# A two-layer encoder on one core: operands padded to multiples of 256 bytes, and softmax steps of paired heads in another order

## The chip, the cores and the metric

The kernel runs on one core of a Trainium2 chip. Its time is device microseconds (us) of that core. The shares, waits and durations below come from one profiled execution, as its own time says.

## What is computed

The reference is an encoder trunk of two layers on 512 tokens of width 1024, all in float32. Layer 0 mixes tokens by dilated attention in three groups, layer 1 by a bidirectional state-space layer; each is followed by a SwiGLU feed-forward of 2816 hidden units.

```python
def reference(x, ...):
    h = x
    for layer in range(DEPTH):                       # DEPTH = 2
        if layer % 2 == 0:
            h = h + dilated_attention_mixer(rms_norm(h, attn_norm), w_qkv, w_attn_out)
        else:
            h = h + s5_mixer(rms_norm(h, ssm_norm), w_ssm_in, ..., w_glu)
        h = h + swiglu_ffn(rms_norm(h, ffn_norm[layer]), w_ffn_in[layer], w_ffn_out[layer])
    return rms_norm(h, final_norm)
```

Attention has 16 heads of 64. For each head and group a banded softmax gives an output and a log-sum-exp; the groups' outputs are weighted by a softmax over the log-sum-exps and added.

## The kernel before

Every large product is three float32r matmuls: an operand is split in a high and a low part, and high x high, high x low and low x high are added in PSUM. `WStream` loads the weights in units of 128x1024 (512 KB); for each unit ScalarE writes the high part `whi` (L111) and VectorE the low part `wlo` (L112), up to two units ahead of their use. `gemm_a` (L742) then runs 24 matmuls of 128x512 for a unit, with the weights stationary and the activations moving: `X` (attention input and, later, attention output), `Y` (input of both feed-forwards and of the state-space layer), `hh`/`hl` in `hid0`, `yh`/`yl` in the pool `ssm`. Two places turn it round, with the weights moving: `emit_v` (L844, 256 columns) and the last product (L1511, 512 columns, with `hh`/`hl` of `hid1` stationary). By the code there are 5,280 float32r matmuls of 512 columns: 1,536 over `X` (64 units), 2,304 over `Y` (96 units), 528 over `hid0`, 384 over `ssm`, 528 at L1511; and 1,152 of 256 columns (768 at L844, 384 in attention).

Tiles come from pools on two sides of each partition. The left side grows up from `const`, with `w` (the weight units), `attn`, `Y`, `e1` and `hid1` behind it; the right side grows down from its top, with `hT` first and `X`, `hid0` and `ssm` below it. By the allocation of the kernel before, tiles of `w`, `attn` and `Y` start 96 bytes past a multiple of 256, those of `X`, `hid0` and the operands in `ssm` 224 bytes, and those of `hid1` 160 bytes.

Attention runs beside the projection of the next head pair. `plan` lists spans of projections: `qk` (7 units of 24 matmuls) and `v`. Each span has a list of pieces, (cost, function), and `Bg.tick` issues the next piece when the credit that the matmuls have earned passes half of its cost; the credit for a matmul is the span's total cost over its matmul time. So a piece's place in program order follows from the costs ahead of it. For an even head h and the odd h + 1, `A` holds the scores (`sc1` for group 1, `sc2` for groups 2 and 3 of both heads; each with the reductions of L892 and L913 on VectorE and the exponentials of L924 on ScalarE). `W` holds the four steps of `weigh`: part 0 is 16 small copies on GpSimd (L936), part 1 is three VectorE instructions (L941, L942) and an exponential, part 2 is four small VectorE instructions (L947 to L949) and the four scalings of `P2` (L951), part 3 is four scalings of `P1` on ScalarE (L954). `B` transposes the probabilities on TensorE (`tr`; L970 reads `P2`, L965 `P1`) and multiplies them by the values (`pv`, L989 and L1000). In the spans 2, 3, 6 and 9 (pairs that start with heads 0, 2, 6 and 10) scores and values of a pair share one span; the pairs 4, 8 and 12 have their scores in a `v` span and their values in the `qk` span behind it; the pair of heads 14 and 15 ends in `tailp`, whose first five pieces stand between the splits of the attention output (`xo`, L1072 on ScalarE and L1073, on GpSimd but for the first) and the rest beside its product (L1092).

Beside the first feed-forward (about 700 to 1,100 us) the same pieces mechanism builds the tables of the state-space layer on VectorE and GpSimd, with transposes at L445.

Of the kernel before, what the change touches and what calls it, by code (L numbers as in the profile page):

```python
# [7 lines left out]
F32 = mybir.dt.float32  # L8
# [5 lines left out]
P = 128  # L14
# [52 lines left out]
def fv(ap):  # L67
    return ap.bitcast(F32)
# [444 lines left out]
def build(tc, a, out):  # L513
# [62 lines left out]
    with ExitStack() as ctx:  # L576
        left = ctx.enter_context(tc.tile_pool(name="const", bufs=1, side="left"))
        wpool = ctx.enter_context(tc.tile_pool(name="w", bufs=3, side="left"))
        right = ctx.enter_context(tc.tile_pool(name="hT", bufs=1, side="right"))
# [13 lines left out]
        hT = [right.tile([P, S], F32, name=f"h{m}") for m in range(KT)]  # L593
        cols = left.tile([P, 64], F32, name="cols")

        def norm_tile(pool, i, m, src_psum=None):

            src = hT[m] if src_psum is None else src_psum
            hi = pool.tile([P, S], F32R, tag=f"hi{m}", name=f"xhi{m}")
            lo = pool.tile([P, S], F32R, tag=f"lo{m}", name=f"xlo{m}")  # L600
            nc.scalar.activation(out=hi, in_=src, func=ACTF.Copy, scale=gains[:, gcol[i], m:m + 1])
            nc.vector.scalar_tensor_tensor(out=lo, in0=src, scalar=gains[:, gcol[i], m:m + 1], in1=fv(hi),  # L602
                                           op0=ALU.mult, op1=ALU.subtract)
            return hi, lo
# [89 lines left out]
        for m in range(KT):  # L694
            if m == 5:
                ps = pso.tile([P, 2, S], F32, tag="o", name="xps")[:, 0, :]
            else:
                pool, tag = ((pss, "s"), (pst, "pt"), (psg, "g"), (pss, "s"))[m // 2]
# [175 lines left out]
        def sc1(h, bp):  # L874
            c = head(h)
            p, e = h // 2, h % 2
            QA, QB, QL = qk[p]["Q"]
            KK = qk[p]["K"][e]
            QQ, QL = (QA, QB)[e], QL[e]
            ps = pss.tile([P, 2, 256], F32, tag="s", name="sps")  # L880
            for j in range(2):
                b = 2 * bp + j
                i0, step = win[b]

                def kap(t):
                    return bass.AP(tensor=t.tensor, offset=t.offset + i0, ap=[list(t.ap[0]), [step, 2], [128, 4], [1, 32]])
                nc.tensor.matmul(ps[:, j, :], QQ[:, b * 128:(b + 1) * 128], kap(KK), start=True, stop=False)

                nc.tensor.matmul(ps[:, j, :], QL[:, b * 128:(b + 1) * 128], kap(KK), start=False, stop=True)
            for j in range(2):  # L890
                b = 2 * bp + j
                nc.vector.tensor_tensor_reduce(out=c.P1[:, b, :], in0=ps[:, j, :], in1=dist1[:, (0, 1, 1, 2)[b], :],  # L892
                                               scale=-SLOPES[h], scalar=-3e38, op0=ALU.add, op1=ALU.max,
                                               accum_out=c.st[:, b:b + 1])
            fin(c, c.P1, 2 * bp, 0)

        def sc2(p, rp):

            cc = [head(2 * p + e) for e in range(2)]
            q = qk[p]  # L900
            pp = [pss.tile([P, 2, 256], F32, tag="s", name="sps") for e in range(2)]
            for j in range(2):
                r = 2 * rp + j
                cs = slice(r * 128, (r + 1) * 128)
                for i, (nq, nk) in enumerate((("q2", "k2"), ("q3", "k3"))):
                    for e in range(2):
                        rows = slice(64 * e, 64 * e + 64)
                        nc.tensor.matmul(pp[e][:, j, 128 * i:128 * i + 128], q[nq][rows, cs], q[nk][rows, cs],
                                         start=True, stop=True)
            for e, c in enumerate(cc):  # L910
                for j in range(2):
                    r = 2 * rp + j
                    nc.vector.tensor_tensor_reduce(out=c.P2[:, r, :], in0=pp[e][:, j, :], in1=dist23,  # L913
                                                   scale=-SLOPES[2 * p + e], scalar=-3e38, op0=ALU.add, op1=ALU.max,
                                                   accum_out=c.st[:, 4 + r:5 + r])
                fin(c, c.P2, 2 * rp, 4)
# [39 lines left out]
        def tr(h, t):  # L956
            c = head(h)
            ps = pst.tile([P, S], F32, tag="pt", name="ptp")
            if t < 2:
                pv = ps.rearrange("p (t r b i) -> p t r b i", t=2, r=4, b=2)  # L960
                for u in range(2):
                    m = 2 * t + u
                    bs = ((m, 1), (m + 1, 0)) if m < 3 else ((0, 0), (3, 1))
                    for x, (b, half) in enumerate(bs):
                        nc.tensor.transpose(pv[:, u, :, x, :], c.P1[:, b, half * 128:half * 128 + 128], ident)  # L965
            else:
                for u in range(2):
                    r = 2 * (t - 2) + u
                    for g in range(2):
                        nc.tensor.transpose(ps[:, u * 256 + g * 128:u * 256 + g * 128 + 128],  # L970
                                            c.P2[:, r, g * 128:g * 128 + 128], ident)
            PT = ap_.tile([P, 2, S], F32R, tag="PT", name="PT", bufs=3)
            nc.scalar.activation(out=PT[:, 0, :], in_=ps, func=ACTF.Copy)  # L973
            nc.vector.tensor_tensor(out=PT[:, 1, :], in0=ps, in1=fv(PT[:, 0, :]), op=ALU.subtract)  # L974
            c.PT[t] = PT
# [33 lines left out]
        def A(h):  # L1009
            s = [(600, lambda: sc1(h, 0)), (600, lambda: sc1(h, 1))]  # L1010
            t = [(1200, lambda i=i: sc2(h // 2, i)) for i in range(2)]
            return s if h % 2 else [s[0], t[0], s[1], t[1]]

        def W(h):
            return [(c, lambda i=i: weigh(h, i)) for i, c in enumerate((1500, 1000, 1500, 1200))]

        def B(h):
            return [(700, lambda: tr(h, 2)), (700, lambda: tr(h, 3)), (700, lambda: tr(h, 0)), (600, lambda: pv(h, 2)),
                    (700, lambda: tr(h, 1)), (600, lambda: pv(h, 3)), (600, lambda: pv(h, 0)), (1000, lambda: pv(h, 1))]

        def mix(x, y):

            n = min(len(x), len(y))
            return [p for q in zip(x, y) for p in q] + x[n:] + y[n:]

        def scores(h):
            w, x = W(h), A(h + 1)
            return A(h) + [w[0], x[0], w[1], x[1], w[2], w[3]]

        def values(h):  # L1030
            return mix(B(h), W(h + 1)) + B(h + 1)

        spans = [[], [], scores(0) + values(0), scores(2) + values(2), scores(4), values(4), scores(6) + values(6),
                 scores(8), values(8), scores(10) + values(10), scores(12), values(12), A(14)]
        for st, pieces in zip(plan, spans):
            if st[0] == "qk":
                bg.span(pieces, 24 * MM * (st[3] - st[2]))
# [31 lines left out]
        def xo(m, eng):  # L1069
# [2 lines left out]
            nc.scalar.activation(out=hi, in_=oT[m], func=ACTF.Copy)  # L1072
            eng.tensor_tensor(out=lo, in0=oT[m], in1=fv(hi), op=ALU.subtract)  # L1073
            XO[m] = (hi, lo)
        tailp = mix(W(14), A(15)) + values(14)
        for m in range(KT - 1):
            xo(m, nc.gpsimd if m else nc.vector)
            if m < 5:
# [152 lines left out]
        sp = s0.enter_context(tc.tile_pool(name="ssm", bufs=1, side="right"))  # L1231
# [1 line left out]
        pY = s0.enter_context(tc.tile_pool(name="psY", bufs=2, space=PSUM))  # L1233
        pT = s0.enter_context(tc.tile_pool(name="psT", bufs=1, space=PSUM))
        p1 = s0.enter_context(tc.tile_pool(name="ps1", bufs=2, space=PSUM))
        Us = [sp.tile([P, 8, 66], F32, name=f"U{i}") for i in range(3)]
        for t in Us:
            nc.vector.memset(t[:, :, 0:1], 0.0)
            nc.vector.memset(t[:, :, 65:66], 0.0)
# [211 lines left out]
        e1 = f1.enter_context(tc.tile_pool(name="e1", bufs=1, side="left"))  # L1451
# [31 lines left out]
                nc.gpsimd.tensor_tensor(out=hv, in0=hv, in1=gfin[0], op=ALU.mult)  # L1483

        def fin_tok(q):
            sc = e1.tile([P, 8], F32, tag="fs", name="fs", bufs=2)
            y, r_, t = (sc[:, i:i + 1] for i in range(3))
            nc.vector.scalar_tensor_tensor(out=y, in0=ssum[:, q, 1:2], scalar=-0.5 / D, in1=ssum[:, q, 0:1],
                                           op0=ALU.mult, op1=ALU.add)
            nc.vector.tensor_scalar(out=r_.bitcast(I32), in0=y.bitcast(I32), scalar1=-0.5, scalar2=GUESS,  # L1490
                                    op0=ALU.mult, op1=ALU.add)
            for _ in range(3):
                nc.vector.scalar_tensor_tensor(out=t, in0=r_, scalar=y, in1=r_, op0=ALU.mult, op1=ALU.mult)
                nc.vector.scalar_tensor_tensor(out=r_, in0=t, scalar=1.5, in1=r_, op0=ALU.add, op1=ALU.mult)
            h0, h1 = (hrow[q][:, i * S:i * S + S] for i in range(2))
            nc.scalar.activation(out=h0, in_=h0, func=ACTF.Copy, scale=r_)
            nc.vector.scalar_tensor_tensor(out=h1, in0=h1, scalar=r_, in1=gfin[1], op0=ALU.mult, op1=ALU.mult)
            for l in range(2):
                nc.sync.dma_start(out=ov[2 * q + l], in_=hrow[q][64 * l:64 * l + 64, :])

        NK = HT // 2
        for fh in range(2):
# [11 lines left out]
            for kp in range(NK - last):  # L1514
                w = ws.get()
# [36 lines left out]
```

## Time and profile before

| | us |
|---|---|
| median of 3 runs | 1680.38 |
| their range | 1677.62 to 1685.16 |
| profiled execution, its own time | 1683.88 |
| its span, first to last instruction | 1682.1 |

TensorE's matmuls cover 93% of the span, VectorE 60%, ScalarE 39%, GpSimd 31%. A matmul's busy time reaches past the start of the next one, since matmuls are pipelined; how fast they follow each other is read from the distance of their starts, or from their count in a stretch that holds nothing else. The granted clock of TensorE is a share of full speed: 1.00 is 2.4 GHz, and near 0.5 is 1.2 GHz.

### The profile page before, as it was taken

Reading aid. Unit: us, or ns where it says so; the run is one execution under the profiler, and the core shown is the slowest. Engines: PE = TensorE matmul, PEld = TensorE weight load, DVE = VectorE, ACT = ScalarE, POOL = GpSimd, SP = SyncE. Lnnn points to the kernel's source line nnn. Section 1 sums busy time; section 2 is a strip of 40 time slices with the busy share of each in tenths; the row PEclk is TensorE's granted clock in tenths of the full one; section 3 lists DMA queues with packets and bytes.
Section 4 is the critical chain, followed back from the end, with each engine's and each line's share of the span. In section 5 each row is a group of like instructions: output and inputs, shape, how many; then the busy total and the mean of one; then the engine's idle time right before and its main releaser. Section 6 shows DMA issues by size and latency. Waiting matters only on the chain. (4 is left out here: it accounts for less than half of the span.)

```text
span 1682.1 us, 22587 instructions
## 1 busy us (share of the span) xinstructions
PE 1557.8 (93%) x8428; PEld 1278.0 (76%) x8428; DVE 1014.1 (60%) x1714; ACT 653.7 (39%) x1148; POOL 524.8 (31%) x788
## 2 busy tenths in 40 slices
PE   8988999999999899999988989888699999999997
PEld 6877888798797678776766767666578888888886
DVE  6366565565556688886777785568845434433223
ACT  5255454454454432344444443422133333332122
POOL 1022011010110340398888986344412110111010
PEclk9999999999999999999998999989899999999999
DMA  6222232222222142345655545658633233333332
GB/s 177 88 63 63 63 89 63 70 70 76 76 63 76 29 109 85 106 118 171 179 132 159 157 127 157 206 187 237 190 85 93 86 101 100 93 89 107 102 100 63
DMA packets 278669, 185.17 MB, mean 110 GB/s; under 512 B 39424, under 2 KB 260768, under 8 KB 276512
## 3 DMA queue, kind: packets, MB, share of 16 engines
q1 hardware_dynamic: 278128, 183.13, 37.3%
q8 instruction: 66, 1.08, 0.3%
q10 hardware_dynamic: 432, 0.60, 0.1%
q14 instruction: 43, 0.35, 0.1%
HBM read 154.34 MB, written 27.26 MB: 108 GB/s over the span
## 5 line engine op out<-in xcount | busy, mean ns | idle before, releaser
L112 DVE TENSOR_TENSOR wlo<-wraw,whi 128x1024 fp32r<-128x1024 f32 (+1 forms) x234 | 302.1, 1294 | 189.9 <-ACT whi L111 184.3
L111 ACT ACTIVATE whi<-wraw 128x1024 fp32r<-128x1024 f32 x238 | 241.5, 1019 | 260.5 <-PE ops L1511 76.3
L742 PE MATMUL gps<-xhi,whi 128*128 128x512 f32 x792 | 322.3, 407 | 0.0
L742 PE MATMUL gps<-xhi,wlo 128*128 128x512 f32 x792 | 313.9, 396 | 0.7 <-DVE wlo L112 0.7
L742 PE MATMUL gps<-xlo,whi 128*128 128x512 f32 x792 | 313.8, 396 | 0.5 <-DVE xlo L602 0.5
L936 POOL COPY st<-st 32x4 f32<-32x4 f32 x256 | 62.1, 243 | 475.8 <-ACT P L924 351.3
L742 PEld LDWEIGHTS gps<-xhi,wlo 128*128 128x128 f32 x792 | 150.7, 190 | 35.1 <-DVE wlo L112 1.2
L742 PEld LDWEIGHTS gps<-xhi,whi 128*128 128x128 f32 x792 | 151.4, 191 | 29.0 <-issue 1.5
L742 PEld LDWEIGHTS gps<-xlo,whi 128*128 128x128 f32 x792 | 151.1, 191 | 27.3 <-DVE xlo L602 0.8
L742 PE MATMUL ups<-xhi,whi 128*128 128x512 f32 x352 | 141.9, 403 | 0.0
L742 PE MATMUL ups<-xhi,wlo 128*128 128x512 f32 x352 | 139.2, 395 | 1.0 <-DVE wlo L112 1.0
L742 PE MATMUL ups<-xlo,whi 128*128 128x512 f32 x352 | 139.1, 395 | 0.0
L1150 POOL TENSOR_TENSOR u<-u,g 128x512 f32<-128x512 f32 x22 | 28.4, 1289 | 214.1 <-DVE u L1148 202.2
L924 ACT ACTIVATE P<-P,st 128x256 f32<-128x256 f32 x128 | 63.8, 499 | 61.4 <-DVE st L921 61.2
L974 DVE TENSOR_TENSOR PT<-ptp,PT 128x512 fp32r<-128x512 f32 x64 | 44.1, 689 | 60.0 <-ACT PT L973 59.8
L742 PEld LDWEIGHTS ups<-xhi,whi 128*128 128x128 f32 x352 | 67.5, 192 | 15.7 <-issue 2.3
L742 PEld LDWEIGHTS ups<-xhi,wlo 128*128 128x128 f32 x352 | 67.3, 191 | 15.9 <-DVE wlo L112 1.5
L1147 ACT ACTIVATE g<-g 128x512 f32<-128x512 f32 x44 | 27.8, 631 | 129.5 <-DVE g L1146 129.4
L742 PEld LDWEIGHTS ups<-xlo,whi 128*128 128x128 f32 x352 | 67.6, 192 | 13.4
L742 PE MATMUL fps<-hh,whi 128*128 128x512 f32 x176 | 73.4, 417 | 0.0
L844 PE MATMUL vps<-whi,xhi 128*128 128x256 f32 x256 | 73.2, 286 | 0.0
L742 PE MATMUL fps<-hh,wlo 128*128 128x512 f32 x176 | 71.3, 405 | 1.5 <-DVE wlo L112 1.5
(318 smaller groups left out, 3263.2 us busy)
## 6 DMA issues: line engine op xcount, KB each, us to landing
wraw<-in_w_ffn_in SPq DMA_DIRECT2D x88, 512.0 KB, 3.9
wraw<-in_w_qkv SPq DMA_DIRECT2D x72, 512.0 KB, 3.7
wraw<-in_w_ffn_out SPq DMA_DIRECT2D x38, 512.0 KB, 3.9
BD<-B SPq DMA_DIRECT2D x16, 512.0 KB, 3.3
TinD<-Tt SPq DMA_DIRECT2D x16, 512.0 KB, 2.6
Ti<-TinD SPq DMA_DIRECT2D x8, 1024.0 KB, 7.1
Bt<-BD SPq DMA_DIRECT2D x8, 1024.0 KB, 7.2
wraw<-in_w_glu SPq DMA_DIRECT2D x64, 128.0 KB, 3.7
```

Of the source, the lines that this page charges most:

```text
L111: nc.scalar.activation(out=hv, in_=wv, func=ACTF.Copy)
L112: self.lo_engine.tensor_tensor(out=lv, in0=wv, in1=fv(hv), op=ALU.subtract)
L742: nc.tensor.matmul(dst, w[:, kt, :], x, start=(start and kt == ks[0] and j == 0), stop=(stop and kt == ks[-1] and j == 2))
L844: nc.tensor.matmul(ps[rp][:, r % 2, :], x, w[:, kk, :], start=(kt == 0 and j == 0 and r % 2 == 0), stop=(kt == 7 and j == 2 and r % 2 == 1))
L924: nc.scalar.activation(out=Pt[:, j, :], in_=Pt[:, j, :], func=ACTF.Exp, bias=st[:, 32 + off + j:33 + off + j], accum_out=st[:, 8 + off + j ...
L936: nc.gpsimd.tensor_copy(par[32 * z:32 * z + 32, y, :, :], own[32 * y:32 * y + 32, z, :, :])
L974: nc.vector.tensor_tensor(out=PT[:, 1, :], in0=ps, in1=fv(PT[:, 0, :]), op=ALU.subtract)
L1147: nc.scalar.activation(out=g, in_=g, func=ACTF.Silu)
L1150: eng.tensor_tensor(out=u, in0=u, in1=g, op=ALU.mult)
```

## The change

Two tiles that nothing uses are allocated behind `cols`, 160 bytes on the left side and 224 bytes on the right. The three `U` tiles get 2304 bytes each instead of 2112, with the same contents. The eight columns of scratch of the last normalization (`fs`, two tiles of 32 bytes in `e1`) move into free columns of `cols`. In attention, parts 0 and 1 of the odd head's `weigh` move from among the values (behind `tr(h, 2)`) to the end of the scores (behind parts 2 and 3 of the even head). For the last pair, `sc1(14, ·)` moves one span up, the scores of head 15 and part 0 for head 14 move from the tail to the span ahead of it, and part 0 and 1 for head 15 move up in the tail.

```diff
         cols = left.tile([P, 64], F32, name="cols")
+        left.tile([P, 40], F32, name="padl")
+        right.tile([P, 56], F32, name="padr")
...
         def scores(h):
             w, x = W(h), A(h + 1)
-            return A(h) + [w[0], x[0], w[1], x[1], w[2], w[3]]
+            v = W(h + 1)
+            return A(h) + [w[0], x[0], w[1], x[1], w[2], v[0], w[3], v[1]]
 
         def values(h):
-            return mix(B(h), W(h + 1)) + B(h + 1)
+            return mix(B(h), W(h + 1)[2:]) + B(h + 1)
 
         spans = [[], [], scores(0) + values(0), scores(2) + values(2), scores(4), values(4), scores(6) + values(6),
-                 scores(8), values(8), scores(10) + values(10), scores(12), values(12), A(14)]
+                 scores(8), values(8), scores(10) + values(10), scores(12), values(12) + A(14)[0::2],
+                 A(14)[1::2] + W(14)[:1] + A(15)]
...
-        tailp = mix(W(14), A(15)) + values(14)
+        w, v = W(14), W(15)
+        tailp = [w[1], v[0], w[2], v[1], w[3]] + values(14)
...
-        Us = [sp.tile([P, 8, 66], F32, name=f"U{i}") for i in range(3)]
+        Us = [sp.tile([P, 576], F32, name=f"U{i}")[:, 0:528].rearrange("p (g j) -> p g j", g=8) for i in range(3)]
...
-            sc = e1.tile([P, 8], F32, tag="fs", name="fs", bufs=2)
+            sc = cols[:, 40 + 8 * (q % 2):48 + 8 * (q % 2)]
```

## Rows read from the trace of the kernel before

**Rows 1.** The page's head and its first part: busy us, share, instructions.

```profile
span 1682.1 us, 22587 instructions
PE 1557.8 (93%) x8428; PEld 1278.0 (76%) x8428; DVE 1014.1 (60%) x1714; ACT 653.7 (39%) x1148; POOL 524.8 (31%) x788
```

**Rows 2.** Windows of 100 us: length, busy of PE, PEld, DVE, ACT, POOL, clock, DMA.

```profile
100.00:200.00 100.00, 90.74 (x473) 75.29 (x472) 59.12 (x143) 47.51 (x99) 13.38 (x47) 0.95 0.23 67
...
700.00:800.00 100.00, 89.49 (x446) 68.33 (x445) 78.14 (x85) 42.16 (x77) 87.55 (x129) 0.97 0.48 138
...
1500.00:1600.00 100.00, 100.00 (x437) 81.69 (x436) 32.30 (x34) 24.97 (x28) 6.46 (x5) 1.00 0.34 104
```

**Rows 3.** Windows filled by one product, L742 over Y, over ssm; then L1511.

```profile
630.00:680.00 50.00, 50.00 (x222) 41.41 (x221) 1.00 0.31 90
1250.00:1285.00 35.00, 35.00 (x152) 28.36 (x151) 1.00 0.35 98
...
1580.00:1640.00 60.00, 60.00 (x259) 48.35 (x258) 1.00 0.32 97
```

**Rows 4.** The costliest groups, by line: busy us, mean ns; here for the counts.

```profile
L742 PE MATMUL gps<-xhi,whi 128*128 128x512 f32 x792 | 322.3, 407 | 0.0
...
L742 PE MATMUL fps<-hh,whi 128*128 128x512 f32 x176 | 73.4, 417 | 0.0
L844 PE MATMUL vps<-whi,xhi 128*128 128x256 f32 x256 | 73.2, 286 | 0.0
```

**Rows 5.** Timeline of PE near 101 us: start, length, instruction, [idle before <- releaser].

```profile
99.71 0.39 PE L742 MATMUL gps<-xlo,whi 128*128 128x512 f32 x1
...
101.33 0.40 PE L742 MATMUL gps<-xhi,wlo 128*128 128x512 f32 x1
105.87 1.11 PE L970 MATMUL ptp<-cst,P 128*128 128x128 f32 x4 [4.14 <-DVE P L951]
...
107.63 0.63 PE L742 MATMUL gps<-xhi,wlo 128*128 128x512 f32 x1
...
110.62 0.53 PE L742 MATMUL gps<-xhi,whi 128*128 128x512 f32 x1
```

**Rows 6.** The window just behind that wait, columns as in rows 2.

```profile
106.70:111.00 4.30, 4.30 (x13) 3.38 (x12) 2.11 (x3) 2.06 (x4) 0.00 (x0) 0.51 0.28 82
```

**Rows 7.** Who waited for whom on PE, whole span: total us, times, longest.

```profile
PE tps L445 <- DVE Tn L417: 33.7, 19, 5.6
PE yps L1317 <- POOL x L1295: 29.9, 14, 5.5
PE ptp L970 <- DVE P L951: 20.4, 6, 4.1
PE sps L908 <- DVE st L892: 5.3, 8, 1.5
```

**Rows 8.** Timeline of ACT, DVE and POOL during the wait of rows 5.

```profile
102.50 1.06 ACT L111 ACTIVATE whi<-wraw 128x1024 fp32r<-128x1024 f32 x1
...
103.59 1.25 DVE L112 TENSOR_TENSOR wlo<-wraw,whi 128x1024 fp32r<-128x1024 f32 x1 [0.33 <-ACT whi L111]
104.76 0.22 DVE L947 TENSOR_TENSOR st<-st 128x4 f32<-128x4 f32 x2
...
105.46 1.14 DVE L951 TENSOR_SCALAR P<-P,st 128x256 f32<-128x256 f32 x4
...
101.36 4.76 POOL L936 COPY st<-st 32x4 f32<-32x4 f32 x13 [0.31 <-ACT P L924]
```

**Rows 9.** Timeline of POOL and PE in the tail, 548 to 560 us.

```profile
551.99 3.83 POOL L1073 TENSOR_TENSOR olo<-oT,ohi 128x512 fp32r<-128x512 f32 x3 [0.53 <-ACT ohi L1072]
555.76 3.67 POOL L936 COPY st<-st 32x4 f32<-32x4 f32 x16
...
553.46 0.69 PE L970 MATMUL ptp<-cst,P 128*128 128x128 f32 x2 [3.79 <-DVE P L951]
...
558.37 0.39 PE L1092 MATMUL aps<-olo,whi 128*128 128x512 f32 x1
```

## The prediction

> **What bounds the kernel now.** I read the page's head first: TensorE is covered 93% of the span, the next engine, VectorE, 60% [rows 1]. Then the windows of 100 us: in attention (100 to 200 us) matmuls cover 91 of 100 us with VectorE at 59; while tables are built (700 to 800) VectorE has 78 and GpSimd 88; in the second feed-forward (1,500 to 1,600) TensorE is covered all the time and VectorE, next, has 32 [rows 2]. So TensorE sets the time outside the tables and the state-space layer, and there two things cost it: how fast matmuls follow each other, and stops.
>
> **How fast they follow.** In a stretch of one product the distance of starts is the stretch plus the last one's 0.39 us, divided by the count. It gives 50.39/222 = 227.0 ns over `Y`, 35.39/152 = 232.8 over `ssm`, 60.39/259 = 233.2 at L1511 [rows 3]; over `X` seven distances take 1.62 us, 231.4 [rows 5]. All have 512 columns, the same type and a granted clock of 1.00, 2.4 GHz, at which the columns alone take 512/2.4 = 213.3 ns. Where the clock stands at 0.51, 1.2 GHz [rows 6], seven distances take 2.99 us, 427 ns each [rows 5]: exactly 512/1.2, nothing on top. So 14 to 20 ns are lost per matmul, only at full clock, and it looks like what feeds the array, not the array. What differs between the products is where the operands lie: both at 96 bytes (`Y`) is the cheapest, 96 against 224 (`X`, `ssm`) costs 5 to 6 ns more, 96 against 160 (L1511) 6 more. That addresses matter is thus shown; that 0 is better than 96 for both is not.
>
> The Trainium skill, page "TensorE: Matmul & The Clock Gate", section "Back-to-back issue gap", gives columns/2.4 + 2.5 ns for a warm matmul, 215.8 ns here; no row shows that figure, and by it the saving below would be about 73 us where I take 51.
>
> **Stops.** PE's waits put 33.7 us on L445 and 29.9 on L1317 (tables and state space, untouched), 20.4 on L970 waiting for L951, six times, 5.3 on L908 [rows 7]. The timeline shows one of the six: transposes of the even head's `P2` come up behind the matmul of 101.33 and run at 105.87, 4.14 us late [rows 5]. They wait for part 2 of the same head, whose instructions stand on VectorE behind the split L112 of the next unit, which waits for L111 on ScalarE; L947 starts at 104.76, the scalings L951 at 105.46 [rows 8]. Behind the stop the clock falls to 1.2 GHz [rows 6], and ten matmuls cost 0.427 instead of 0.232: 2.0 us more.
>
> **The change, part by part.** *Pads.* Left tiles move by 160 bytes, right ones by 224 down; `hid1` loses the 64 bytes of `fs` below it. Everything that stood at 96, 160 or 224 is then at 0. Large matmuls by the code: `gps` three times 792, 1,320 of them `X` and 1,056 `Y`, with three times 176 over `hid0`, three times 256 for L844 [rows 4]; in all 2,304 over `Y`, 2,448 over `X`, `hid0` and `ssm`, 528 at L1511, 1,152 of 256 columns. What a matmul costs with both at 0 no row shows. Floor: 213.3. Ceiling: 227.0, since equal places are the cheapest seen; above it only by a reason that the rows don't give. I take the middle, 220: 2,304 x 7.0 = 16.1, 2,448 x 12 = 29.4 (from 232), 528 x 13.2 = 7.0. For the 256-column ones I have no clean stretch; half of the 12 ns each, 6.9, bounds 0 and 13.8. Sum 59.4 us. Not all of it ends the program earlier: while tables are built, GpSimd at 88 and VectorE at 78 of 100 us [rows 2] keep their own time and L445 waits the longer. I let half go there (1,056 x 7.0 + 528 x 12, halved: 6.9) and all of `w_ssm_in` (192 x 7.0 = 1.3), beside which VectorE sets the pace. Left: **51 us**; with 213.3 it is 87, with 227.0 it is 15.
>
> *Order.* In the four shared spans the pieces cost 26,400 against 7 x 24 x 216 = 36,288 ns of matmuls, so with the 1.02 of the planner 0.742 credit a ns. Parts 0 and 1 of the odd head, 2,500, now lie between part 2 of the even head and `tr(h, 2)`: 2,500/0.742 = 3.4 us of matmuls at 216, 3.4 to 3.6 at the real pace. That is work PE does instead of standing: of 4.14 us some 0.6 is left. Whether the clock then holds no row says; of its 2.0 us I take 1.4 as saved. With 3.5 that is 4.9 each, 19 in all; bounds 8 (half the cover, the clock falling as before) and 25 (all of 4.14 and 2.0). Nothing is added: the same instructions run. Moved up, the 16 copies of part 0 stand on GpSimd, otherwise idle in attention (13 of 100 us [rows 2]); they already ran early, done at 106.12 [rows 8]. Part 1 now stands on VectorE ahead of the next evacuations and the next split, and waits for those copies: covered as long as they end before L951 does, 106.60 here; beyond it VectorE and the split behind it wait.
>
> *Tail.* Part 0 of head 15, 3.67 us on GpSimd, passes from behind the six `olo` subtractions to behind the first of them; the low halves (1.28 us each [rows 9]) are what the second pass of L1092 reads. In return part 0 of head 14 and all scores run a span earlier, so GpSimd starts this list some 4 us earlier and ends it about when it does now. PE loses the 3.79 us stop at 553.46 [rows 9] but then reaches `olo` sooner and waits for it in part. I take 4 us saved, bounds 0 and 6. `sc2` of heads 14 and 15 stand next to each other and fight for two PSUM buffers: 0 to 1.5 us once [rows 7], inside those bounds. `U` tiles and `fs` cost nothing: the same instructions in the same order on the same engines.
>
> **Sum.** 51 + 19 + 4 = 74 off the profiled execution's 1,683.9: 1,610. That execution is 3.5 above the median of the runs, so **1,606**.
>
> **Rivals.** *Only the relation counts*: both at the same place cost 227, wherever it is. For it: the classes differ by relation, and nothing at 0 was seen. Against it: 13.7 ns over the columns still lacks a reason. 15 + 23 = 38: 1,642. *Addresses do nothing*, the classes differing for another cause (which engines run beside); against it, that L1511, in the stretch where the least else runs (1,500 to 1,600 [rows 2]), is the dearest [rows 3]. 23 alone: 1,657. On this the Trainium skill, page "SBUF — State Buffer", section "Specifications (TRN2)", says that what counts is 16-byte lines; 96, 160 and 224 are all multiples of 16, so by it the pads would bring nothing. The rows disagree, 227 against 233. *The stops stay*, since part 2 is held by L112 and ScalarE and not by its place, while the pads work: 1,606 + 23 = 1,629. *A new stop, slower*: part 1 of the odd head reaches VectorE before GpSimd's copies are done; the split L112 and PSUM evacuations queue behind it, and PE stands at the next unit. It decides once the copies end later than VectorE gets there by more than the lead of the split, about one unit (24 x 0.232 = 5.6 us). Eight pairs, up to the 4.76 us of the copies [rows 8] and 1.4 of clock each, 50 us; with pads that bring nothing and the 23 saved: 1,683.9 + 27 - 3.5 = 1,707. Against it: copies done at 106.12, VectorE there at 106.60; but in `v` spans the pieces run closer and the margin is not seen.
>
> **How the numbers follow.** Forecast 0.55; only the relation 0.22; addresses nothing 0.08; the stops stay 0.06; the new stop 0.09, of which 0.04 with about half its price, near no change. The forecast's own bounds run from 213.3 (1,570) to where the second case begins, 1,642. The range takes the second case in and ends at the third: 1,576 to 1,657; outside it remain the new stop, the edge of the third and the very floor. Faster by over 0.5%, about what a measurement of this kernel can tell from no change (below 1,672): 0.91; within 0.04; slower 0.05.
>
> **What would show it.** Counts of matmuls in stretches of one product: 50 us over `Y` should hold about 229 instead of 222, 60 us of L1511 about 274 instead of 259; if the three classes agree at 227 ns, the relation was all; if they still differ, addresses were nothing. In PE's waits the line L970 <- L951 should fall from 20.4 to under 5 us and the clock in attention rise; L941 on VectorE waiting for L936 by microseconds would be the new stop, and L445 <- L417 growing by several us the part that tables take back. The prediction is wrong at its largest term if matmuls with both operands at 0 are no faster than at 96, or if far more than half is lost beside the tables.

## The result, and the profile after

The changed kernel takes **1661.7 us** (median, 1659.84 to 1663.72), against 1682.1 for the kernel before beside it: a ratio of 0.9881, 95% interval 0.9853 to 0.9908. A second series gave 0.9880 (0.9864 to 0.9897). It is faster, by 20 us or 1.2%; the prediction had said 76 off, 1606, and its range ended at 1657. Of what it wanted to see, two things came: the four stops in the shared spans are nearly gone, and the three products that it wanted counted run at one pace. But that pace is the 227 ns that `Y` already had, and TensorE stops longer in the tail.

The page of after begins so; it answers to [rows 1]:

```profile
span 1660.7 us, 22585 instructions
PE 1542.7 (93%) x8428; PEld 1273.7 (77%) x8428; DVE 1009.8 (61%) x1714; ACT 652.5 (39%) x1148; POOL 522.9 (31%) x788
```

Windows of after, columns as in [rows 2]; the first three answer to [rows 2], the last to [rows 6]:

```profile
100.00:200.00 100.00, 96.52 (x563) 81.32 (x562) 65.68 (x175) 52.73 (x120) 13.91 (x50) 1.00 0.25 74
700.00:800.00 100.00, 93.25 (x472) 72.13 (x471) 78.09 (x86) 44.27 (x80) 89.21 (x119) 0.98 0.51 146
1500.00:1600.00 100.00, 100.00 (x443) 82.81 (x442) 34.15 (x35) 26.94 (x34) 10.20 (x8) 1.00 0.32 100
106.70:111.00 4.30, 4.30 (x24) 3.57 (x24) 2.87 (x8) 2.66 (x7) 0.20 (x1) 1.00 0.42 122
```

In attention TensorE is covered 96.52 instead of 90.74 of 100 us, and where the clock stood at 0.51 behind the stop, with 13 matmuls in 4.3 us, it is now 1.00, with 24. The stop itself, [rows 5], in the timeline of after (the lines moved by three: L970 is L973, L951 is L954):

```profile
105.36 0.39 PE L745 MATMUL gps<-xhi,wlo 128*128 128x512 f32 x1
106.64 0.59 PE L973 MATMUL ptp<-cst,P 128*128 128x128 f32 x3 [0.89 <-DVE P L954]
```

0.89 us where 4.14 stood; the other three left 0.68 to 0.70 where 3.93 to 3.95 stood. Windows of one product, TensorE alone (length, busy and count, clock, DMA), to hold against [rows 3]: L745 over `Y`, over `ssm`, and L1517 (before: L1511):

```profile
1490.00:1530.00 40.00, 40.00 (x178) 1.00 0.31 93
1245.00:1280.00 35.00, 35.00 (x156) 1.00 0.35 97
1560.00:1620.00 60.00, 60.00 (x266) 1.00 0.30 97
```

By the prediction's own rule that is 40.39/178 = 226.9, 35.39/156 = 226.9 and 60.39/266 = 227.0 ns, where before had 227.0, 232.8 and 233.2. The rule is coarse, since one matmul more or less in the count is 0.9 to 1.5 ns; the mean distance of the starts themselves in these stretches is 226.7 in all three, and before it was 226.7, 232.4 and 233.3. And TensorE's waits over the whole span, against [rows 7]:

```profile
PE tps L445 <- DVE Tn L417: 36.9, 17, 5.7
PE yps L1323 <- POOL x L1301: 31.3, 16, 5.6
PE aps L1098 <- ACT ohi L1077: 6.0, 3, 2.7
PE ptp L973 <- DVE P L954: 5.6, 5, 2.7
```

The wait for part 2 fell from 20.4 to 5.6 us, of which 2.7 are in the tail. The third line, also in the tail, grew; in the kernel before it was

```profile
PE aps L1092 <- ACT ohi L1072: 2.7, 2, 1.6
```

Where the time went, by stages (us from the start of the first matmul of one stage to that of the next, in the last row to the start of the last matmul; the columns behind "after" are experiments told below):

| stage | before | after | pads only | order only | all at 96 | old tail | copies early | tail early | difference of 32 |
|---|---|---|---|---|---|---|---|---|---|
| attention | 540.7 | 524.1 | 539.1 | 524.3 | 538.2 | 521.7 | 525.0 | 528.4 | 539.2 |
| attention output (tail) | 64.2 | 66.3 | 64.7 | 67.9 | 64.5 | 65.0 | 61.1 | 57.2 | 64.2 |
| first feed-forward, tables | 464.4 | 466.7 | 461.4 | 466.9 | 464.2 | 462.8 | 464.6 | 461.3 | 466.1 |
| state space, `w_glu` | 230.5 | 225.1 | 226.6 | 230.7 | 226.1 | 228.3 | 226.6 | 226.3 | 229.5 |
| second feed-forward, in | 245.2 | 245.1 | 245.1 | 245.2 | 245.1 | 245.1 | 245.1 | 245.1 | 251.6 |
| last product | 123.0 | 119.5 | 119.5 | 123.0 | 119.5 | 119.5 | 119.5 | 119.5 | 123.0 |

The last two rows hardly scatter. The table stage does: without any pad it stands at 464.4 and 466.9, with pads at 461.3 to 466.7, so single differences of 3 us in that row say nothing. Attention scatters too: a second profile of the changed kernel, told below, has 521.8 there and 67.0 in the tail.

### The profile page after: what moved, and what is told of

The parts are those of the page before. It is cut to its first block, busy times and chain, and to the rows that moved or that the text cites. A ratio compares the mean times of both kernels' runs of the same rounds, so it can differ in the third digit from the quotient of the medians.

```text
span 1660.7 us, 22585 instructions
## 1 busy us (share of the span) xinstructions
PE 1542.7 (93%) x8428; PEld 1273.7 (77%) x8428; DVE 1009.8 (61%) x1714; ACT 652.5 (39%) x1148; POOL 522.9 (31%) x788
## 5 line engine op out<-in xcount | busy, mean ns | idle before, releaser
L745 PE MATMUL gps<-xhi,whi 128*128 128x512 f32 x792 | 320.3, 404 | 0.0
L745 PE MATMUL gps<-xhi,wlo 128*128 128x512 f32 x792 | 311.9, 394 | 0.8 <-DVE wlo L112 0.8
L745 PE MATMUL gps<-xlo,whi 128*128 128x512 f32 x792 | 311.2, 393 | 0.5 <-DVE xlo L605 0.5
L745 PEld LDWEIGHTS gps<-xhi,wlo 128*128 128x128 f32 x792 | 149.8, 189 | 34.3 <-DVE wlo L112 1.3
L745 PEld LDWEIGHTS gps<-xhi,whi 128*128 128x128 f32 x792 | 150.2, 190 | 27.9 <-issue 1.8
L745 PEld LDWEIGHTS gps<-xlo,whi 128*128 128x128 f32 x792 | 150.4, 190 | 26.4 <-DVE xlo L605 0.8
L745 PE MATMUL ups<-xhi,whi 128*128 128x512 f32 x352 | 141.6, 402 | 0.0
L745 PE MATMUL ups<-xhi,wlo 128*128 128x512 f32 x352 | 139.0, 395 | 1.0 <-DVE wlo L112 1.0
L745 PE MATMUL ups<-xlo,whi 128*128 128x512 f32 x352 | 139.1, 395 | 0.0
L927 ACT ACTIVATE P<-P,st 128x256 f32<-128x256 f32 x128 | 63.8, 499 | 70.3 <-DVE st L924 70.1
L745 PEld LDWEIGHTS ups<-xhi,whi 128*128 128x128 f32 x352 | 67.6, 192 | 15.7 <-issue 2.3
L745 PEld LDWEIGHTS ups<-xhi,wlo 128*128 128x128 f32 x352 | 67.2, 191 | 15.9 <-DVE wlo L112 1.5
L745 PEld LDWEIGHTS ups<-xlo,whi 128*128 128x128 f32 x352 | 67.4, 192 | 13.4
L847 PE MATMUL vps<-whi,xhi 128*128 128x256 f32 x256 | 73.3, 286 | 0.0
L745 PE MATMUL fps<-hh,whi 128*128 128x512 f32 x176 | 72.9, 414 | 0.0
L847 PE MATMUL vps<-whi,xlo 128*128 128x256 f32 x256 | 72.4, 283 | 0.0
L847 PE MATMUL vps<-wlo,xhi 128*128 128x256 f32 x256 | 72.4, 283 | 0.0
```

The lines of the kernel that those rows point to most:

```text
L745: nc.tensor.matmul(dst, w[:, kt, :], x, start=(start and kt == ks[0] and j == 0), stop=(stop and kt == ks[-1] and j == 2))
L847: nc.tensor.matmul(ps[rp][:, r % 2, :], x, w[:, kk, :], start=(kt == 0 and j == 0 and r % 2 == 0), stop=(kt == 7 and j == 2 and r % 2 == 1))
L927: nc.scalar.activation(out=Pt[:, j, :], in_=Pt[:, j, :], func=ACTF.Exp, bias=st[:, 32 + off + j:33 + off + j], accum_out=st[:, 8 + off + j ...
```

## The experiments

The theory after the result: what counts is how far apart the starts of a matmul's two operands lie, modulo 256 bytes, and 227 ns is the price at distance 0 wherever they are; the order gave what the prediction said, except in the tail, where the first link of the rival "a new stop" came true in one place.

**The pads alone.** The old order, with the pads, the `U` tiles of 576 columns and the `fs` columns:

```diff
+        left.tile([P, 40], F32, name="padl")
+        right.tile([P, 56], F32, name="padr")
...
-        Us = [sp.tile([P, 8, 66], F32, name=f"U{i}") for i in range(3)]
+        Us = [sp.tile([P, 576], F32, name=f"U{i}")[:, 0:528].rearrange("p (g j) -> p g j", g=8) for i in range(3)]
...
-            sc = e1.tile([P, 8], F32, tag="fs", name="fs", bufs=2)
+            sc = cols[:, 40 + 8 * (q % 2):48 + 8 * (q % 2)]
```

> The pads, the U tiles of 576 columns and the fs columns alone, in the old order. Theory A (what counts is how far apart the starts of a matmul's two operands lie, modulo 256 bytes; equal starts cost 227 ns wherever they lie): starts of the 512-column matmuls follow each other after 226.7 ns over X, Y, hid0, ssm and in the last product alike; the stops of 4 us in the shared spans stay; the pace gives some 2.5 us in attention, 3 in ssm and 3.5 in the last product, nothing in the table stage: 1,671 to 1,675 us, 7 to 11 below before. Rival B (the order is worth the 23 us that the prediction gave it, the pads hardly anything, because the old order hid the gain): within 3 us of before.

Measured: 1672.1 us, ratio 0.9955 (0.9936 to 0.9973), so 7.6 us by the ratio. Over `ssm` and in the last product, columns as in [rows 2]:

```profile
1255.00:1290.00 35.00, 35.00 (x156) 29.01 (x155) 18.86 (x18) 11.68 (x14) 9.75 (x8) 1.00 0.32 93
1580.00:1640.00 60.00, 60.00 (x266) 49.72 (x266) 17.38 (x16) 14.48 (x20) 5.04 (x4) 1.00 0.28 88
```

226.9 and 227.0 ns. The stops stay, by TensorE's waits:

```profile
PE ptp L973 <- DVE P L954: 20.8, 6, 4.3
```

The rival that the pads give hardly anything falls: its time of no change lies outside the interval. The gain is not that of the `U` tiles or of `fs`: two kernels below have the same of both and no equal starts in these products, and their matmuls are no faster there than before.

**The order alone.** Tiles where they were, the new lists:

```diff
-            return A(h) + [w[0], x[0], w[1], x[1], w[2], w[3]]
+            v = W(h + 1)
+            return A(h) + [w[0], x[0], w[1], x[1], w[2], v[0], w[3], v[1]]
...
-            return mix(B(h), W(h + 1)) + B(h + 1)
+            return mix(B(h), W(h + 1)[2:]) + B(h + 1)
```

and the last two spans and the tail list of the change.

> The new order alone, tiles where they were before. Theory A (the order takes the four stops of 4 us and the low clock behind them away, and the new tail gives 2 us back): matmuls over ssm stay at 232 ns and in the last product at 233 ns, PE's wait for part 2 (the line that evacuates tr) falls to about 1 us each, 1,670 to 1,674 us. Rival B (the prediction's 19 and 4): 1,657 to 1,660 us. The sum of this run's gain and that of the pads alone should be the 20 us of the whole change if the two don't touch each other.

Measured: 1671.8 us, ratio 0.9931 (0.9913 to 0.9949), 11.6 us. The paces are those of before, 60 us of the last product again hold 259:

```profile
1580.00:1640.00 60.00, 60.00 (x259) 1.00 0.27 88
```

and TensorE's waits are those of after:

```profile
PE aps L1095 <- ACT ohi L1074: 6.5, 3, 2.7
...
PE ptp L970 <- DVE P L951: 4.7, 5, 2.7
```

7.6 and 11.6 make 19.2 of the 20.0 of the whole change: within their intervals, some 3 us each, the two parts add up. In the stage table the order saves 16.4 in attention and loses 3.7 in the tail; the four stops alone make 13 of the 16.4.

**Everything at 96.** Does it take multiples of 256? The old order with a right pad alone, so that every large operand, `hid1` too, starts at 96 modulo 256:

```diff
-        left.tile([P, 40], F32, name="padl")
-        right.tile([P, 56], F32, name="padr")
+        right.tile([P, 32], F32, name="padr")
```

> Old order; only the right side is moved, by a pad of 128 bytes, so that every operand of the large matmuls, hid1 too, starts at 96 modulo 256 instead of at 0. Theory A (the distance of the two starts decides): 226.7 ns in all classes and the time of the kernel with the pads alone, within 3 us. Rival C (multiples of 256 themselves are needed): 229 ns or more over X, ssm and in the last product, and a time no more than 4 us below before.

Measured: 1675.5 us, ratio 0.9961 (0.9948 to 0.9974), beside 0.9955 for the pads alone; by the medians the two lie 3.4 us apart, a little more than the 3 expected, by the ratios 1. Over `ssm` and in the last product:

```profile
1255.00:1290.00 35.00, 35.00 (x156) 1.00 0.36 100
1580.00:1640.00 60.00, 60.00 (x267) 1.00 0.29 94
```

226.9 and 226.2 ns by the count, 226.7 in both by the starts. Multiples of 256 do nothing of their own; equal starts do. In this kernel the starts over `ssm` lie 256 apart modulo 512, so equality modulo 256 is enough. The Trainium skill, page "SBUF — State Buffer", section "Specifications (TRN2)", speaks of 16-byte lines; every start in all these kernels is a multiple of 16, and still the prices differ.

**Other distances.** The kernel before with small pads at three places, which shift `Y`, `ssm` and `hid1` against the weights:

```diff
+        Yp.tile([P, 8], F32, name="pady")
         acc = Yp.tile([P, S], F32, tag="acc", name="acc", bufs=1)
...
+                if 2 * t2 + gp == 7:
+                    sp.tile([P, 8], F32, name="pads")
```

with `U` and `fs` as in the change; in the second kernel the pads are 16 and 56 columns, and 24 ahead of `hid1`.

> The kernel before with pads of 32 bytes ahead of Y's tiles and 32 behind those of the state-space stage, so that the starts of moving and stationary operand differ by 32 bytes over Y (before: 0), by 96 over ssm (before: 128) and by -32 in the last product (before: -64), all modulo 256. Theory A (any difference costs, only equal starts are cheap): 231 to 234 ns in all three. Rival G (only the larger differences cost): 227 to 229 ns over Y and in the last product. Beside the tables the same 1,030 products over Y get some 5 us dearer as in the second feed-forward. If the tables and not the matmuls set the time there, the table stage grows by less than 2 us and the program by 5 to 8 us, to 1,687 to 1,690; if matmuls set it, the stage grows by 5 and the program by 11, to 1,692.

> As the scan before, with differences of 64 bytes over Y, of 160 over ssm and of -160 (that is 96) in the last product. Theory A: 231 to 234 ns in all three, the 96 of the last product like the 96 over ssm, since it would not matter which of the two operands lies ahead. Rival G: 64 near 227 to 229.

The first, over `Y`, `ssm` and in the last product, TensorE alone:

```profile
1512.00:1552.00 40.00, 40.00 (x173) 1.00 0.29 84
...
1262.00:1297.00 35.00, 35.00 (x152) 1.00 0.32 91
...
1590.00:1650.00 60.00, 60.00 (x259) 1.00 0.30 91
```

and the second, in the same order of products:

```profile
1508.00:1548.00 40.00, 40.00 (x176) 1.00 0.31 92
...
1255.00:1290.00 35.00, 35.00 (x151) 1.00 0.38 104
...
1580.00:1640.00 60.00, 60.00 (x259) 1.00 0.32 96
```

With [rows 3] this is the whole list in steps of 32 (start of the moving operand less that of the stationary one, modulo 256), by the count and in brackets by the mean distance of the starts: 0 costs 226.9 ns (226.7), 32: 233.5 (233.3), 64: 229.5 (228.9), 96: 232.8 over `ssm` and 233.2 in the last product (233.3 in both), 128: 232.8 (232.4), 160: 234.4 (234.3), 192: 233.2 (233.3), 224: 233.2 (233.3). Every distance but 0 costs 2 to 8 ns more; 64 is the cheapest of them, for which I have no reason. That any difference costs stands, but not that all cost the same: at 64 the rival's 227 to 229 was the better figure. The second kernel ran once, 1684.4 us.

The first of the two also answers how much the tables hide. Over `Y` the products became 6.7 ns dearer, 1,056 of them in each feed-forward, 7.0 us. The second one grew by 6.4 us (245.2 to 251.6), the first, beside the tables, by 1.7. TensorE's wait there takes up a part of the difference, 30.8 us for the 33.7 of [rows 7]:

```profile
PE tps L445 <- DVE Tn L417: 30.8, 18, 5.5
```

The program took 1688.9 us, ratio 1.0038 (1.0023 to 1.0053), 6.4 more: what the second feed-forward lost. So beside the tables the pace of the matmuls is worth little, a quarter here and with the scatter of that stage perhaps nothing.

**Where the 13.3 ns come from.** At 2.4 GHz 512 columns are 213.3 ns; 226.7 leaves 13.3. With the pads, the last product with both operands as 2-byte numbers, which lowers its precision:

```diff
+            half = self.ns >= len(self.units) - HT
+            if half:
+                hi, lo = hi.bitcast(BF16), lo.bitcast(BF16)
...
+                if pool_mult:
+                    hi, lo = (t.bitcast(BF16)[:, 0:S] for t in (hi, lo))
```

> The kernel with the pads alone, but the 528 products of the last stage take both operands as 2-byte numbers, at the same starts (this lowers the precision of that product). Theory A' (the 13.3 ns that are left over the columns at equal starts come from reading 4-byte operands): the distance of starts falls to 216 ns or below, the last stage from 119.5 to 114 us. Rival H (they belong to every matmul of 512 columns at full clock, whatever its type): 226 to 227 ns, 119.5 us.

Busy of TensorE, then of its weight load, in 60 us of that product:

```profile
1580.00:1640.00 60.00, 60.00 (x279) 27.20 (x278) 18.97 (x17) 14.48 (x20) 4.96 (x4) 1.00 0.27 88
```

279 matmuls instead of 266, 60.39/279 = 216.5 ns; the stage took 113.8 us from the first to the last of 528 starts, 215.9 for each of 527 distances. So 2.5 of the 13.3 ns are left, and the other 11 belong to 4-byte operands, not to every matmul. A weight load takes 27.20/278 = 98 ns instead of 49.72/266 = 187; whether the weight load or the moving operand makes the difference stays open, since both were halved. One number leans to a price for each matmul and not for each column: the 4-byte matmuls of 256 columns at L847 of after follow each other after 120 ns in the median, again 13 over their 106.7. The kernel ran once, 1667.4 us.

**The old tail.** The changed kernel, its last two spans and its tail list as before:

```diff
-                 scores(8), values(8), scores(10) + values(10), scores(12), values(12) + A(14)[0::2],
-                 A(14)[1::2] + W(14)[:1] + A(15)]
+                 scores(8), values(8), scores(10) + values(10), scores(12), values(12), A(14)]
...
-        tailp = [w[1], v[0], w[2], v[1], w[3]] + values(14)
+        tailp = mix(W(14), A(15)) + mix(B(14), W(15)) + B(15)
```

> The changed kernel with its pads and its order in the shared spans, but the last two spans and the tail list of the kernel before. Theory A (the new tail is the place where the rival of the new stop came true: VectorE's part 1 of head 15 waits 2.8 us for GpSimd's copies and the evacuations of oT behind it hold TensorE): 2 to 5 us faster than the changed kernel, about 1,657 to 1,660 us. Rival D (the new tail is as good as the old one, and what it shows of stops the old tail has elsewhere): within 1.5 us of the changed kernel, 1,660 to 1,663 us. The prediction's 4 us for the tail would give 1,666 us.

Measured: 1657.6 us, ratio 0.9853 (0.9839 to 0.9868), 4 us faster than the change. The two intervals overlap a little, but of eight runs of the change in two series the fastest took 1658.0, and of the four here the slowest 1658.3: the new tail costs time. The timeline of after shows one way, GpSimd, VectorE, ScalarE and TensorE (the copies are part 0 of head 15, L944 and L945 its part 1, `ohi` and `olo` the copies of `oT` for the attention output):

```profile
532.00 3.74 POOL L939 COPY st<-st 32x4 f32<-32x4 f32 x16
535.82 2.49 POOL L1078 TENSOR_TENSOR olo<-oT,ohi 128x512 fp32r<-128x512 f32 x2
...
535.77 1.33 DVE L944 TENSOR_TENSOR st<-st 128x4 f32<-128x4 f32 x2 [2.79 <-POOL st L939]
537.14 1.20 DVE L945 TENSOR_SCALAR st<-st 128x8 f32<-128x8 f32 x1
...
538.37 0.21 ACT L946 ACTIVATE st<-st 128x8 f32<-128x8 f32 x1 [6.69 <-DVE st L945]
538.49 0.61 ACT L1077 ACTIVATE ohi<-oT 128x512 fp32r<-128x512 f32 x1
...
539.15 0.80 PE L1098 MATMUL aps<-ohi,whi 128*128 128x512 f32 x1 [2.37 <-ACT ohi L1077]
```

VectorE reaches part 1 of head 15 and waits 2.79 us for the copies; ScalarE stands 6.69 us at the exponential behind it, L946, and behind that in its queue stands the next `ohi`, which doesn't need it; TensorE waits 2.37 us for that `ohi`. The first link, VectorE held by copies that come too late, is the rival's, in the one place where GpSimd has other work ahead of the copies; from there the wait runs over ScalarE, not over a split or an evacuation.

It isn't the only one. Of TensorE's 6.0 us for `ohi` 2.72 pass before these copies begin, at the first `ohi`:

```profile
527.70 0.49 ACT L927 ACTIVATE P<-P,st 128x256 f32<-128x256 f32 x1
528.19 0.61 ACT L1077 ACTIVATE ohi<-oT 128x512 fp32r<-128x512 f32 x1
...
528.86 0.50 PE L1098 MATMUL aps<-ohi,whi 128*128 128x512 f32 x1 [2.72 <-ACT ohi L1077]
532.26 1.11 PE L973 MATMUL ptp<-cst,P 128*128 128x128 f32 x4 [2.66 <-DVE P L954]
```

On ScalarE it stands right behind the exponentials (L927) of head 15's scores, which the change moved to the end of the last `v` span; before, TensorE waited 1.15 us there. And the stop for part 2 of head 14, 3.79 us in [rows 9], is still 2.66.

**Copies early, tail early.** To test that, one piece alone is moved: part 0 of head 15 to the end of the last `v` span. And a larger step: all four parts of head 14 and parts 0 and 1 of head 15 go there. First the changed kernel itself beside them:

> The changed kernel itself, as the measure beside its two other tails on the same chip: 1,660 to 1,664 us.

```diff
-                 A(14)[1::2] + W(14)[:1] + A(15)]
+                 A(14)[1::2] + W(14)[:1] + A(15) + W(15)[:1]]
...
-        tailp = [w[1], v[0], w[2], v[1], w[3]] + values(14)
+        tailp = [w[1], w[2], v[1], w[3]] + values(14)
```

> The changed kernel with one piece moved: part 0 of head 15, with its 16 copies on GpSimd, goes from the tail list to the end of the last span of v, ahead of the subtractions for olo. Theory A: the wait of 2.8 us of VectorE's part 1 of head 15 for these copies is gone, and the time falls by 2 to 4 us, to 1,658 to 1,660 us. Rival F (TensorE's stops in the tail come from part 2 of head 14 and the low clock, not from the copies): within 1.5 us of the changed kernel.

```diff
-                 A(14)[1::2] + W(14)[:1] + A(15)]
+                 A(14)[1::2] + W(14)[:1] + A(15) + mix(W(14)[1:], W(15)[:2])]
...
-        tailp = [w[1], v[0], w[2], v[1], w[3]] + values(14)
+        tailp = values(14)
```

> The changed kernel, but all four softmax parts of head 14 and parts 0 and 1 of head 15 run in the last span of v, ahead of the copies of oT; the tail list is values(14) alone. Theory A (the new tail loses because the 16 copies of head 15 on GpSimd stand between the olo subtractions, and VectorE's part 1, and behind it ScalarE's copies ohi, wait for them): VectorE's wait at part 1 of head 15 is gone, TensorE's wait for ohi falls from 6.0 to under 3 us, 1,653 to 1,657 us. Rival E (the softmax work only moves and the last span of v, or the first product of the attention output, takes the same microseconds elsewhere): 1,660 to 1,664 us.

Measured: the change 1660.8 us (0.9880, 0.9864 to 0.9897), copies early 1656.4 (0.9852, 0.9838 to 0.9865), tail early **1654.6** (0.9847, 0.9828 to 0.9867). With the copies early, GpSimd and VectorE:

```profile
526.32 3.45 POOL L939 COPY st<-st 32x4 f32<-32x4 f32 x13 [0.30 <-ACT P L927]
529.85 2.52 POOL L1078 TENSOR_TENSOR olo<-oT,ohi 128x512 fp32r<-128x512 f32 x2
...
529.89 1.33 DVE L944 TENSOR_TENSOR st<-st 128x4 f32<-128x4 f32 x2
531.26 1.13 DVE L945 TENSOR_SCALAR st<-st 128x8 f32<-128x8 f32 x1
```

The wait of 2.79 us is gone. TensorE:

```profile
529.24 0.95 PE L973 MATMUL ptp<-cst,P 128*128 128x128 f32 x4 [3.76 <-DVE P L954]
...
535.33 0.50 PE L1098 MATMUL aps<-ohi,whi 128*128 128x512 f32 x1 [1.39 <-ACT ohi L1077]
```

Behind the copies its waits for `ohi` fall from 2.37 and 0.90 us to 1.39. The two waits ahead of them, 2.72 and 2.66, have become one of 3.76, since with one piece more in the `v` span six matmuls of the projection now stand behind the last scores, where none did. The time falls by 4.4 us where 2 to 4 were expected; the intervals of the change and of copies early just touch. That the late copies cost TensorE time is thus shown, by the waits behind them, which shrink by 1.9 us when they are moved; how the rest of the 4.4 divides is not. With the tail early no wait for `ohi` is among the larger ones; a wait of 4.9 us for an evacuation takes its place:

```profile
PE ptp L968 <- DVE PT L977: 4.9, 1, 4.9
```

yet the tail is shorter by 9.1 us than in the change and attention longer by 4.3, since the work now stands there. It is the fastest version that ran, 26 us below the kernel before by the ratio; that it beats copies early is not shown, the intervals overlap.

## Why the prediction was wrong

**What bounds the kernel, and which classes differ:** right. The cheap class was the one with equal starts, and the pads brought the products over `ssm` and the last one to its price.

**The pace at 0 taken as 220 ns:** wrong, and the largest error. It was the middle between the columns alone and the cheapest row seen, and it came out at the ceiling, 226.9. No row stood below 227, and the rival "only the relation counts" described what happened; I gave it 0.22, against 0.55 for a forecast that rested on the 13.7 ns over the columns having no other reason. Most of them have one, the operands' width. By terms: `Y` 16.1 us forecast, 0 measured (245.2 to 245.1 in the second feed-forward); the last product 7.0, 3.5 measured.

**The products over `X`:** 1,320 of the 2,448 in the second term. Clean stretches reach the new price (in after, 32 distances of starts from 98.10 to 105.36 us, 226.9 each), but attention as a whole gained little: 1.6 us with the pads alone, and 2.1 in the mean of three profiles with the old order and equal starts (539.1, 538.2 and 537.0, the last from the 2-byte kernel) against three without (540.7, 539.2, and 540.7 in the second of the other distances). Of three products in a row the first, in front of which the pieces of the other heads come, shows why: the distance from its start to the next goes from 232 to 227 ns in the median where no piece stands ahead (295 of 440), but from 234 to 239 where one does. The rival's 15 us for the pads (14 by its own terms, 12.2 + 3.3 - 1.3) were too high for this reason among others; 7.6 (4.5 to 10.8) were measured.

**256 columns:** 6.9 forecast, 0 measured: over all of L844 the median distance of starts was 119 ns before and 120 after, though the distance modulo 256 went from 128 to 0 there too. Why half the columns show no effect stays open.

**Half lost beside the tables:** too little, as far as the runs can tell. The stage shows no gain beyond its scatter, and L445 waits 36.9 us instead of 33.7, as foretold for the part that tables take back; but the order alone, without pads, also shows 36.3, so that wait alone proves nothing. The kernel with `Y` made dearer says more: of 7.0 us 1.7 reached the stage, which alone is within its scatter, but the program lost 6.4 (3.9 to 8.9) and not the 14 of both feed-forwards.

**The order in the shared spans:** right. 19 us forecast; attention lost 16.4 in the run with the order alone, and the old tail, which has this order and the pads but not the new tail, stands 17 us below the pads alone by the ratios (0.9955 less 0.9853), 14.5 by the medians. The stop shown left 0.89 us where 0.6 was said, and behind it the clock held at 1.00, where I had counted on 1.4 of the 2.0 us.

**The tail:** 4 us gain forecast, a loss of some 4 measured. The prediction saw both halves, that the 16 copies pass from behind the six `olo` to behind the first, and that part 1 of an odd head waits for them, as a rival for the shared spans; it didn't put them together at the one place where they meet. It took the effect on `olo` for the price; the price was VectorE's wait of 2.79 us and the `ohi` queued behind ScalarE's L946 (2.37 and 0.90 us on TensorE). Two more steps failed: the stop of 3.79 us was taken as gone and stayed at 2.66, and the scores moved ahead of the tail hold the first `ohi`, 2.72 us, a term that the prediction doesn't have.

**Sum:** 59.4 - 8.2 = 51 for the pads became 7.6; 19 + 4 for the order became 11.6. The range's upper end, "addresses do nothing" with the whole 23 of the order, 1,657, held no case in which the tail loses and the pads bring little at once; that is where the time fell. From the rival's 1,642 it is 7 us less from the pads, 8 from the tail and some 3 from the order in the shared spans: about 1,660.

## What to carry to other kernels

Where classes of the same instruction differ in price, moving all to the cheapest class is worth the difference at most; a price that no row shows needs an experiment, not a middle. Before a piece is moved on a queue, list for each of its instructions who waits for it in order on the other engines; here 16 small copies that TensorE doesn't read stopped it over two engines. And price a gain by stage: beside the tables, which other engines pace, slower matmuls cost little of what they cost elsewhere.

## What the runs showed of the hardware

- A matmul of 512 4-byte columns at 2.4 GHz costs 226.7 ns if the starts of both operands are equal modulo 256 bytes, 228.9 to 234.3 at other distances in steps of 32; with 2-byte operands at equal starts 215.9. The Trainium skill, page "TensorE: Matmul & The Clock Gate", section "Back-to-back issue gap", gives columns/2.4 + 2.5 ns, 215.8 here: the 2-byte run agrees, no 4-byte run does. At 1.2 GHz the 4-byte products took 427 ns, nothing over the columns [rows 5].
- VectorE's small steps stretch while GpSimd subtracts: two of 128x4 and one of 128x8 took 0.23 and 0.17 us at 529.45 in after and 1.33 and 1.20 at 535.77, each ending within 0.05 us of one of GpSimd's two subtractions (2.49 us from 535.82, so at 537.07 and 538.31); the same with the copies early (1.33 and 1.13 at 529.89). Not every step waits: with the tail early a reciprocal of 128x8 (L952) took its usual 0.20 us at 535.13, beside a subtraction. The Trainium skill, page "SBUF — State Buffer", section "SBUF: two separate sides", says that these two engines share a pair of ports as a lock for a whole instruction; the rows of these steps agree. That VectorE's part 1 runs beside `olo` thus makes it some 2 us longer. With the tail early it runs ahead of the subtractions and is short again, while part 2 (L950, L951) now runs beside them; VectorE, tail early:

```profile
528.48 0.24 DVE L944 TENSOR_TENSOR st<-st 128x4 f32<-128x4 f32 x2 [1.22 <-POOL st L939]
528.75 0.17 DVE L945 TENSOR_SCALAR st<-st 128x8 f32<-128x8 f32 x1
...
532.54 1.32 DVE L950 TENSOR_TENSOR st<-st 128x4 f32<-128x4 f32 x2
533.89 1.21 DVE L951 TENSOR_TENSOR st<-st 128x8 f32<-128x8 f32 x1
```

What these 2 us are worth in the program's time no run separates.
